# FFN up projections with weights or tokens as the stationary operand

## The chip, the cores and the metric

The kernel runs on one core of a Trainium2 chip. The metric is the device time of one execution in microseconds (us); smaller is better. Before the change it was 1040.62 us, the median of three runs (1040.27 to 1041.07).

## What is computed

Two layers of a decoder trunk, for 256 tokens of 1024 features in float32. Each layer has three sub-layers: an FFN, a token mixer, and another FFN, each behind a norm that a conditioning vector modulates. The FFN is what matters here:

```python
def _swiglu(h, w_up, w_down):          # h [256, 1024], w_up [1024, 2 * 2816], w_down [2816, 1024]
    gu = h @ w_up
    g, u = jnp.split(gu, 2, axis=-1)
    return (jax.nn.silu(g) * u) @ w_down
...
        x = x + 0.5 * gate(0) * _swiglu(norm_mod(x, 0), w_ffn_up[l, 0], w_ffn_down[l, 0])
        x = x + gate(1) * _mixer(norm_mod(x, 1), ...)
        x = x + 0.5 * gate(2) * _swiglu(norm_mod(x, 2), w_ffn_up[l, 1], w_ffn_down[l, 1])
```

## The kernel before

Every float32 matrix product is made of three float32r products: both operands are split into a high part (a cast to float32r) and a low part (what is left), and high x high, high x low and low x high are summed in PSUM. Weights come from HBM in units of 128 x 1024 (`unit`, line 251). ScalarE casts each to `H` (line 247), VectorE subtracts for `L` (line 248). There are 6 buffers for raw units and 11 for split ones. The conditioning (`ada_ss`, `ada_gate`, lines 281 to 323) streams its own weights through VectorE between the chunks of the FFNs.

The normed activations lie transposed in `hTh` and `hTl`: [feature, token tile, feature tile, token], two token tiles of 128.

An FFN has 2816 hidden features, worked on as 11 chunks j of 256. For a chunk and a token tile t, `up(j, t)` (line 466) fills one PSUM bank [128 tokens, 512]: the 256 gate columns and the 256 value columns of the chunk. Its 24 matmuls (8 feature tiles x 3 part products, lines 270 and 272) hold 128 tokens of `hTh` or `hTl` stationary and move 512 weight columns. Silu (line 485) and a product (line 490) give `sg` [128 tokens, 256]. `tr(j, t)` (line 492) transposes it with two matmuls against the identity (line 495, tile `tg`), casts to `gh` (line 498) and subtracts for `gl` (line 499). `down(j, t)` (line 502) then multiplies with two units of down weights: 12 matmuls of 512 columns into two PSUM banks `dn`, which stay open over all chunks (`mm3`, lines 259 to 261). The last chunk's `down` is followed by the residual and the next norm: `norm_sq`, `rsqrt` on GpSimd, `norm_xn` on ScalarE, then transposes `tp` (line 414) and the split of `norm_out`.

In the very first FFN (`pre`), four chunks are begun while the norm's modulation still arrives feature tile by feature tile (line 920); lines 467 to 473 finish them.

The order is written as a list `ops` (lines 523 to 542): an up projection, the transposes of the one before, the down projection of the one before that. At the end it is rearranged so that the first token tile ends early (a = chunk 9, b = chunk 10):

```python
        ops += [(up, (b, 0)), (tr, (a, 1)), (down, (a, 0)), (tr, (b, 0)), (down, (a - 1, 1)), (down, (b, 0)),
                (up, (b, 1)), (tr, (b, 1)), (down, (a, 1)), (lambda *_: after and after[1](0), (0, 0)), (down, (b, 1))]
```

The list is not the order in which the engines work: a scheduler with its own estimate of times orders each engine's queue when the kernel is built, with the list's order as priority. Work that it holds not ready is overtaken by later work. `tc.issue_after(x)` keeps what follows in its block behind x on the engine of x. Each engine then works in order.

Of the kernel before, what the change touches and what calls it, by code (L numbers as in the profile page):

```python
# [9 lines left out]
F32 = mybir.dt.float32  # L10
# [21 lines left out]
# columns of w_in that make up each 512-wide group  # L32
# [7 lines left out]
# tiles of the mixed groups in the order in which they come  # L40
# [33 lines left out]
def _offsets(sizes):  # L74
    at, out = 0, {}
    for name, n in sizes:
# [9 lines left out]
       for n, k in (("cw", 16), ("cb", 4), ("br", 4), ("bi", 4), ("gm", 8), ("wf", 4 * KT))]  # L86
)
CST, N_CST = _offsets([(n, 128) for n in ("ident", "ones", "trif")] + [("fold", 4)]
                       + [(n, 128) for n in ("ntri", "nones", "msb", "mfx")])
# [5 lines left out]
def trunk_kernel(ctx: ExitStack, tc: tile.TileContext, x, c, wst, ada, par, cst, row, bgate, wg, out):  # L95
# [7 lines left out]
    sm = pool("sm", 32)  # L103
    gtp = pool("gtp", 2)
# [26 lines left out]
    # the rows of x, each followed by what adds EPS to its mean square  # L131
# [13 lines left out]
    # -8 * softplus(-lambda), with log1p by its series in e / (2 + e)  # L145
# [27 lines left out]
    # 1/sqrt by two of Newton's steps from a guess on the bits, up to a factor for the user to apply  # L173
# [3 lines left out]
    # the conditioning vector along the rows, and as columns  # L177
# [7 lines left out]
    # for the first norm RS * gain and RS * gain * (1 + bias), by which its scale is one step from its sum  # L185
# [9 lines left out]
    # causal masks next to zeros: [sb | 0 | fox]  # L195
# [4 lines left out]
    def late_constants():  # L200
# [3 lines left out]
        ntri, nones, msb, mfx = (once[:, i * 128:(i + 1) * 128] for i in range(4))  # L204
        S.dma_start(out=r_sb, in_=row.broadcast_to([128, N_ROW]))
        V.tensor_copy(idb, ident)
        for m, n in ((ones_r, C("ones")), (ntri_r, ntri), (nones_r, nones)):
            A.copy(m, n)
# [26 lines left out]
    live = {}  # L235

    # weights not needed at once wait for the norm of the first token tile to be through
# [87 lines left out]
    # in an order in which each is ready when needed, and no gate's row is replaced before its last use  # L325
# [42 lines left out]
    # transposed activations, [feature, token tile, feature tile, token], in their two parts  # L368
# [36 lines left out]
    def norm_out(l, j, t):  # L405
# [4 lines left out]
        for q in range(2):  # L410
# [4 lines left out]
            # one engine per bank  # L415
# [46 lines left out]
    def ffn(l, s, after, pre={}):  # L462
# [3 lines left out]
        def up(j, t):  # L466
            if (j, t) in pre:
                o = pre[j, t]
                wh, wl = unit(("up", l, s, j, KT // 2 - 1))
                for h, w in ((0, wh), (1, wh), (0, wl)):  # L470
                    for i in range(2):
                        T.matmul(o, lhsT=hT[t][h][:, KT - 2 + i, :], rhs=w[:, i * 512:(i + 1) * 512],  # L472
                                 start=False, stop=i == 1 and w is wl)
            else:
                o = PA([128, 512], name="up")
                def w(k):
                    q = slice((k % 2) * 512, (k % 2 + 1) * 512)
                    return [part[:, q] for part in unit(("up", l, s, j, k // 2))]

                if (j, t) == (1, 0):  # L480
                    hold.append(1)
                over_features(o, t, w, (K_T[0 if s else 1], flush) if (j, t) == (1, 0) else None, by=4 if j == 0 else 1)
                hold.clear()
            sg = sgp.tile([128, CH], F32, tag="sg", name="sg")
            silu = act(sg, o[:, 0:CH], AF.Silu)
            prod[j, t] = sg
            if after and (j, t) == (NCH - 1, 1):
                with tc.issue_after(silu.ins):
                    norm_xn(0)
            return V.tensor_tensor(out=sg, in0=sg, in1=o[:, CH:2 * CH], op=ALU.mult)  # L490

        def tr(j, t):
# [7 lines left out]
            gT[j, t] = (gh, gl)  # L500

        def down(j, t):
            if j == 0:
                dn[t] = [PD([128, 512], name="dn") for _ in range(2)]
            gh, gl = gT[j, t]
# [17 lines left out]
        seq = [(0, 0), (1, 0), (0, 1), (1, 1)] + [(j, t) for j in range(2, NCH) for t in range(NT)]  # L523
        if pre:
            seq = [(j, t) for j in range(NCH) for t in range(NT)]
        ops = []
        for i, jt in enumerate(seq):
            ops.append((up, jt))
            if i >= 1:
                ops.append((tr, seq[i - 1]))  # L530
            if i >= 2:
                ops.append((down, seq[i - 2]))
        if pre:
            u, r, d = up, tr, down
            head = [(u, (0, 0)), (u, (0, 1)), (r, (0, 0)), (u, (1, 0)), (r, (0, 1)), (u, (1, 1)), (u, (2, 0)), (u, (2, 1)), (d, (0, 0)), (d, (0, 1)), (r, (1, 0)), (r, (1, 1)), (u, (3, 0)), (d, (1, 0)), (r, (2, 0)), (u, (3, 1)), (d, (1, 1))]
            ops = head + [p for p in ops if p not in head]
        # the first token tile ends early, so that its norm runs under the second's products
        a, b = NCH - 2, NCH - 1
        ops = ops[:ops.index((up, (b, 0)))]
        ops.remove((down, (a - 1, 1)))  # L540
        ops += [(up, (b, 0)), (tr, (a, 1)), (down, (a, 0)), (tr, (b, 0)), (down, (a - 1, 1)), (down, (b, 0)),
                (up, (b, 1)), (tr, (b, 1)), (down, (a, 1)), (lambda *_: after and after[1](0), (0, 0)), (down, (b, 1))]
        for f, jt in ops:
            mul = f(*jt)
            if f is up and jt[1] == 1 and (N_PRE - 1 if pre else 0) < jt[0] < NCH - 1:
                ada_step(ADA_FFN[2 * l + s][jt[0] >= NCH - 4])
            if pre and f is up and jt == (N_PRE, 0):
# [4 lines left out]
    def mixer(l, after):  # L552
# [19 lines left out]
        # RG-LRU: the gelu branch, and the input transposed to [feature, token] with the conv's left margin  # L572
# [12 lines left out]
        # causal conv, gates, log of the decay; two feature tiles at a time  # L585
# [50 lines left out]
            # the queries' scale of HD ** -0.5 goes into the argument  # L636
# [20 lines left out]
        more(fp[:, 4:8], lhsT=C("ones"), rhs=lf[:, 0:4])  # L657
# [15 lines left out]
        # the recurrence  # L673
# [14 lines left out]
        # forgetting attention's scores, [query, key]  # L688
# [34 lines left out]
        # stick-breaking attention  # L723
# [11 lines left out]
        # scores, [key, query], by parity of the head  # L735
# [4 lines left out]
        for e in range(2):  # L740
# [14 lines left out]
            # products with 0 and -1: exact on the two parts  # L755
# [15 lines left out]
        # group norms, then the exact split of the transposed groups  # L771
# [11 lines left out]
        # y of the recurrence: mean square over features by a product with ones  # L783
# [11 lines left out]
        T.matmul(mo, lhsT=C("ones"), rhs=sq[:, 0, :], start=True, stop=True)  # L795
# [11 lines left out]
        # values: [token, head, d]  # L807
# [19 lines left out]
        def values(y, products):  # L827
            """A bank of several sums: the first product opens it, and the others come behind that one."""
# [27 lines left out]
        def finish(t, between=lambda: None):  # L856
            """One bank after the other, so that the residual starts on the first."""
# [23 lines left out]
    # The first layer's shift and scale come feature tile by feature tile, and the first chunks' products  # L881
    # follow them in that order.
# [16 lines left out]
    banks = (PT, PD, PD, PA)  # L899
    for k in range(KT):  # L900
# [9 lines left out]
        for j in range(N_PRE):  # L910
            wh, wl = unit(("up", 0, 0, j, k // 2))
            if k == 1:
                for t in range(NT):
                    pre[j, t] = banks[j]([128, 512], name="up")
            # the parts in the order in which they come about
            for h, w in ((0, wh), (1, wh), (0, wl)):
                for i in range(2):
                    for t in range(NT):
# [101 lines left out]
```

## Time and profile before

| What | Before |
|---|---|
| median of three runs | 1040.62 us |
| the profiled execution, first to last instruction | 1039.9 us |
| instructions | 12805 |
| PE (TensorE matmuls) busy | 1005.7 us, 97% |
| PEld (TensorE weight loads) busy | 803.9 us, 77% |
| DVE (VectorE) busy | 758.1 us, 73% |
| ACT (ScalarE) busy | 534.9 us, 51% |
| bytes read from HBM | 246.15 MB, 238 GB/s over the span |
[...]

PE and PEld are two sides of one engine: a matmul needs its stationary operand loaded, and the load of the next one can run beside the matmul in progress. [...] DVE, ACT and GpSimd (POOL) do everything that is not a matrix product; SP issues the DMAs.

### The profile page before, as it was taken

Reading aid. Unit: us, or ns where it says so; the run is one execution under the profiler, and the core shown is the slowest. Engines: PE = TensorE matmul, PEld = TensorE weight load, DVE = VectorE, ACT = ScalarE, POOL = GpSimd, SP = SyncE. Lnnn points to the kernel's source line nnn. Section 1 sums busy time; section 2 is a strip of 40 time slices with the busy share of each in tenths; the row PEclk is TensorE's granted clock in tenths of the full one; section 3 lists DMA queues with packets and bytes.
Section 4 is the critical chain, followed back from the end, with each engine's and each line's share of the span. In section 5 each row is a group of like instructions: output and inputs, shape, how many; then the busy total and the mean of one; then the engine's idle time right before and its main releaser. Section 6 shows DMA issues by size and latency. Waiting matters only on the chain.

```text
span 1039.9 us, 12805 instructions
## 1 busy us (share of the span) xinstructions
PE 1005.7 (97%) x4542; PEld 803.9 (77%) x4542; DVE 758.1 (73%) x1105; ACT 534.9 (51%) x857; POOL 54.1 (5%) x108
## 2 busy tenths in 40 slices
PE   6999999989999899999999999999999989999998
PEld 4888888768787788888878888887777778888886
DVE  7988877769886797878569887655677559646452
ACT  5473534468775444344455344446679455635340
POOL 1000000120011200000020000001100220000000
PEclk9999999989999999999999999999999999999999
DMA  9989988758473799989539989854542328755511
GB/s 327 375 305 301 339 305 306 263 197 268 148 251 103 242 368 323 318 324 332 195 124 344 337 308 332 311 191 138 184 161 82 101 101 313 272 185 178 187 61 41
DMA packets 68910, 248.04 MB, mean 239 GB/s; under 512 B 7783, under 2 KB 8295, under 8 KB 68846
## 3 DMA queue, kind: packets, MB, share of 16 engines
q1 hardware_dynamic: 68846, 247.23, 67.9%
q8 instruction: 35, 0.57, 0.2%
q14 instruction: 29, 0.24, 0.1%
HBM read 246.15 MB, written 1.05 MB: 238 GB/s over the span
## 4 chain that ended last, share of the span: by engine, by line
PE 82%; ACT 6%; POOL 4%; DVE 4%; issue 3%; DMA 1%; POOLq 0%; ACTq 0%; DVEq 0%
PE up L270 27%; PE up L272 13%; PE dn L259 8%; PE dn L261 8%; PE dn L260 8%; PE pj L270 5%; PE up L920 3%; PE pj L272 2%; PE tg L495 2%; POOL na L359 2%; ACT H L247 2%; POOL ny L360 1%; PE up L472 1%; DVE L L248 1%; PE tp L414 1%
## 5 line engine op out<-in xcount | busy, mean ns | idle before, releaser
L248 DVE TENSOR_TENSOR L<-raw,H 128x1024 fp32r<-128x1024 f32 x320 | 379.0, 1221 | 76.6 <-ACT H L247 74.6
L247 ACT CAST H<-raw 128x1024 fp32r<-128x1024 f32 x320 | 326.8, 1056 | 93.3 <-PE up L272 54.6
L270 PE MATMUL up<-H,hTh 128*128 128x512 f32 x640 | 254.8, 398 | 0.5 <-DVE hTh L427 0.5
L270 PE MATMUL up<-L,hTh 128*128 128x512 f32 x640 | 253.6, 396 | 0.0
L272 PE MATMUL up<-H,hTl 128*128 128x512 f32 x640 | 247.7, 396 | 0.0
L458 ACT ACTIVATE sg<-up 128x256 f32<-128x256 f32 x88 | 33.8, 384 | 242.1 <-PE up L272 237.3
L259 PE MATMUL dn<-H,gh 128*128 128x512 f32 x352 | 146.8, 417 | 2.1 <-ACT gh L498 2.1
L270 PEld LDWEIGHTS up<-H,hTh 128*128 128x128 f32 x640 | 120.9, 189 | 29.5 <-DVE hTh L427 1.3
L272 PEld LDWEIGHTS up<-H,hTl 128*128 128x128 f32 x640 | 120.8, 189 | 29.1
L270 PEld LDWEIGHTS up<-L,hTh 128*128 128x128 f32 x640 | 120.8, 189 | 28.5
L260 PE MATMUL dn<-L,gh 128*128 128x512 f32 x352 | 140.1, 398 | 0.0
L261 PE MATMUL dn<-H,gl 128*128 128x512 f32 x352 | 139.7, 400 | 0.0
L289 DVE SCALAR_TENSOR_TENSOR raw<-raw,cb 128x1024 f32<-128x1024 f32 x96 | 114.2, 1220 | 2.6 <-DMA raw<-in_ada 1.6
L490 DVE TENSOR_TENSOR sg<-sg,up 128x256 f32<-128x256 f32 x88 | 36.9, 420 | 103.7 <-ACT sg L458 103.5
L261 PEld LDWEIGHTS dn<-H,gl 128*128 128x128 f32 x352 | 67.0, 190 | 16.1 <-DVE gl L499 0.2
L259 PEld LDWEIGHTS dn<-H,gh 128*128 128x128 f32 x352 | 66.8, 190 | 15.5 <-ACT gh L498 3.3
L260 PEld LDWEIGHTS dn<-L,gh 128*128 128x128 f32 x352 | 67.3, 191 | 12.9
L270 PE MATMUL pj<-H,hTh 128*128 128x512 f32 x160 | 65.6, 410 | 0.1
L272 PE MATMUL pj<-H,hTl 128*128 128x512 f32 x160 | 65.2, 408 | 0.0
L270 PE MATMUL pj<-L,hTh 128*128 128x512 f32 x160 | 63.9, 399 | 0.0
L312 DVE SCALAR_TENSOR_TENSOR acc<-raw,cs,acc 128x1024 f32<-128x1024 f32 x48 | 61.5, 1283 | 1.1 <-DVE sg L490 0.2
L499 DVE TENSOR_TENSOR gl<-tg,gh 128x256 fp32r<-128x256 f32 x88 | 36.9, 419 | 26.2 <-ACT gh L498 26.2
(252 smaller groups left out, 984.3 us busy)
## 6 DMA issues: line engine op xcount, KB each, us to landing
raw<-in_wst SPq DMA_DIRECT2D x320, 512.0 KB, 5.0
raw<-in_ada SPq DMA_DIRECT2D x144, 512.0 KB, 5.3
x<-in_x SPq DMA_DIRECT2D x2, 512.0 KB, 4.1
wgt<-in_wg SPq DMA_DIRECT2D x2, 512.0 KB
out_x<-x SPq DMA_DIRECT2D x4, 256.0 KB, 2.0
once<-in_cst SPq DMA_DIRECT2D x1, 256.0 KB
p_sb<-in_par SPq DMA_DIRECT2D x1, 148.0 KB
r_sb<-in_row SPq DMA_DIRECT2D x1, 132.0 KB
```

The costliest lines, as they stand in the source:

```text
L247: A.copy(h, raw)
L248: V.tensor_tensor(out=lo, in0=raw, in1=h.bitcast(F32), op=ALU.subtract)
L259: T.matmul(o, lhsT=xh, rhs=wh, start=first, stop=False)
L260: T.matmul(o, lhsT=xh, rhs=wl, start=False, stop=False)
L261: return T.matmul(o, lhsT=xl, rhs=wh, start=False, stop=last)
L270: T.matmul(o, lhsT=hh[:, k, :], rhs=part, start=k == 0 and i == 0, stop=False)
L272: mul = T.matmul(o, lhsT=hl[:, k, :], rhs=w(k)[0], start=False, stop=k == KT - 1)
L289: V.scalar_tensor_tensor(out=raw, in0=raw, scalar=1.0, in1=cb, op0=ALU.mult, op1=ALU.mult, accum_out=st[:, v, k:k + 1])
L312: V.scalar_tensor_tensor(out=acc, in0=raw, scalar=cs[:, m:m + 1], in1=acc, op0=ALU.mult, op1=ALU.add)
L458: used.append(A.activation(*a, **k))
L490: return V.tensor_tensor(out=sg, in0=sg, in1=o[:, CH:2 * CH], op=ALU.mult)
L499: V.tensor_tensor(out=gl, in0=tp, in1=gh.bitcast(F32), op=ALU.subtract)
```

## The change

For most chunks the roles of the operands are exchanged. `up_w(j, i)` holds a 128 x 128 block of weights stationary and moves all 256 tokens: it fills a PSUM bank [128 hidden features, gate and value, 256 tokens], for half i of the chunk's features. It has 48 matmuls (8 feature tiles x 3 part products x gate and value), each of 256 columns. The result is transposed as it comes, so Silu, product, cast and subtraction give `gh` and `gl` [feature, token] without `tr`. `down` is the same but for where it finds its stationary operand.

Chunks 0, 1 and 10 keep `up` and `tr` in three FFNs; in the first FFN only chunk 10 does, and the four early chunks use the new form too. The lists `ops` are written anew, and at the end of an FFN `down(a - 1, 1)` comes ahead of `up(b, 0)`. Two constants (ones, and minus ones) are written by VectorE instead of loaded and copied; the pool `gtp` has 3 buffers for each tag instead of 2, `sm` has 30 instead of 32; the early chunks' PSUM banks come from other pools. `up_w` returns its last matmul where `up` returned VectorE's product, which is what `late_constants` is ordered behind.

```diff
+    def up_part(o, w, kk, v, i, h, k, opens):
+        q = kk * 512 + v * CH + i * 128
+        return T.matmul(o[:, v], lhsT=w[:, q:q + 128], rhs=(hTh, hTl)[h][:, :, k, :], start=opens, stop=True,
+                        skip_group_check=True)
...
+        def up_w(j, i):
+            if (j, i) in pre:
+                o = pre[j, i]
+                wh, wl = unit(("up", l, s, j, KT // 2 - 1))
+                for h, w in ((0, wh), (1, wh), (0, wl)):
+                    for kk in range(2):
+                        for v in range(2):
+                            mul = up_part(o, w, kk, v, i, h, KT - 2 + kk, False)
+            else:
+                o = PA([128, 2, SEQ], name="up")
+                with ExitStack() as behind:
+                    for k in range(KT):
+                        wh, wl = unit(("up", l, s, j, k // 2))
+                        for h, w in ((0, wh), (0, wl), (1, wh)):
+                            for v in range(2):
+                                opens = k == 0 and h == 0 and w is wh and v == 0
+                                mul = up_part(o, w, k % 2, v, i, h, k, opens)
+                                if opens:
+                                    behind.enter_context(tc.issue_after(mul.ins))
+            sg = sgp.tile([128, SEQ], F32, tag="sg", name="sg")
+            act(sg, o[:, 0], AF.Silu)
+            V.tensor_tensor(out=sg, in0=sg, in1=o[:, 1], op=ALU.mult)
+            gh = gtp.tile([128, NT, 128], F32R, tag="gh", name="gh")
+            gl = gtp.tile([128, NT, 128], F32R, tag="gl", name="gl")
+            sg = sg.rearrange("p (t q) -> p t q", t=NT)
+            A.copy(gh, sg)
+            V.tensor_tensor(out=gl, in0=sg, in1=gh.bitcast(F32), op=ALU.subtract)
+            for t in range(NT):
+                gT[j, i, t] = (gh[:, t], gl[:, t])
+            return mul
...
-                mm3(dn[t][n], gh[:, i, :], gl[:, i, :], w[i][0][:, q], w[i][1][:, q],
+                mm3(dn[t][n], *gT[j, i, t], w[i][0][:, q], w[i][1][:, q],
...
+        u, w, r, d = up, up_w, tr, down
         if pre:
+            ops = [(w, (0, 0)), (w, (0, 1)), (w, (1, 0)), (w, (1, 1)), (d, (0, 0)), (w, (2, 0)), (d, (0, 1)),
+                   (w, (2, 1)), (d, (1, 0)), (w, (3, 0)), (d, (1, 1)), (w, (3, 1)), (w, (4, 0)), (d, (2, 0)),
+                   (d, (2, 1)), (w, (4, 1)), (d, (3, 0)), (d, (3, 1))]
+        else:
+            ops = [(u, (0, 0)), (u, (1, 0)), (r, (0, 0)), (u, (0, 1)), (r, (1, 0)), (d, (0, 0)), (u, (1, 1)),
+                   (r, (0, 1)), (d, (1, 0)), (w, (2, 0)), (r, (1, 1)), (d, (0, 1)), (w, (2, 1)), (d, (1, 1))]
         a, b = NCH - 2, NCH - 1
+        for j in range(5 if pre else 3, a):
+            ops += [(w, (j, 0)), (d, (j - 1, 0)), (w, (j, 1)), (d, (j - 1, 1))]
+        ops += [(w, (a, 0)), (d, (a - 1, 0)), (w, (a, 1)), (d, (a - 1, 1)), (u, (b, 0)), (d, (a, 0)), (r, (b, 0)),
+                (d, (b, 0)), (u, (b, 1)), (r, (b, 1)), (d, (a, 1)), (lambda *_: after and after[1](0), (0, 0)),
+                (d, (b, 1))]
         for f, jt in ops:
             mul = f(*jt)
...
-            if pre and f is up and jt == (N_PRE, 0):
+            if f is up_w and pre and jt == (N_PRE, 0):
                 with tc.issue_after(mul.ins):
                     late_constants()
...
-    banks = (PT, PD, PD, PA)
+    banks = (PD, PD, PT, PA)
...
-            for h, w in ((0, wh), (1, wh), (0, wl)):
                 for i in range(2):
-                    for t in range(NT):
-                        kk = k - 1 + i
-                        T.matmul(pre[j, t], lhsT=hT[t][h][:, kk, :], rhs=w[:, i * 512:(i + 1) * 512],
-                                 start=kk == 0 and w is wh and h == 0, stop=kk == KT - 1 and w is wl)
+                    pre[j, i] = banks[j]([128, 2, SEQ], name="up")
+            with ExitStack() as behind:
+                for h, w in ((0, wh), (1, wh), (0, wl)):
+                    for kk in range(2):
+                        for v in range(2):
+                            for i in range(2):
+                                opens = k == 1 and h == 0 and w is wh and kk == 0 and v == 0
+                                mul = up_part(pre[j, i], w, kk, v, i, h, k - 1 + kk, opens)
```

## Rows read from the trace of the kernel before

**Rows 1.** The page: busy us of an engine, share of the span, instructions.
```profile
span 1039.9 us, 12805 instructions
...
PE 1005.7 (97%) x4542; PEld 803.9 (77%) x4542; DVE 758.1 (73%) x1105; ACT 534.9 (51%) x857; POOL 54.1 (5%) x108
```

**Rows 2.** Table by windows: length, busy us and starts by engine, clock, DMA, GB/s.
```profile
26.00:54.00 28.00, 28.00 (x122) 22.72 (x121) 27.66 (x49) 13.10 (x17) 0.00 (x0) 1.00 1.00 377
...
80.00:132.00 52.00, 52.00 (x230) 41.90 (x229) 45.57 (x78) 21.97 (x31) 0.00 (x0) 1.00 0.92 316
```

**Rows 3.** Waits, 80 to 185 us: who waited for whom, us, times, longest.
```profile
ACT sg L458 <- PE up L272: 52.3, 12, 8.0
```

**Rows 4.** Groups by shape, whole run: busy us, mean ns, idle us before.
```profile
L495 PE MATMUL tg<-c_sb,sg 128*128 128x128 f32 x176 | 33.4, 272 | 0.0
...
L229 PE MATMUL s<-mask,idb 128*128 128x512 bf16 x6 | 1.6, 383 | 0.0
```

**Rows 5.** Timeline of PE, first FFN: start us, length us, line, tiles, count.
```profile
61.96 0.40 PE L259 MATMUL dn<-H,gh 128*128 128x512 f32 x1
...
65.94 0.40 PE L261 MATMUL dn<-H,gl 128*128 128x512 f32 x1
...
123.67 0.38 PE L495 MATMUL tg<-c_sb,sg 128*128 128x128 f32 x2
...
132.29 0.38 PE L495 MATMUL tg<-c_sb,sg 128*128 128x128 f32 x2
```

**Rows 6.** Timeline of PE and PEld, 100 to 104 us.
```profile
100.15 0.39 PE L270 MATMUL up<-L,hTh 128*128 128x512 f32 x1
100.15 0.19 PEld L272 LDWEIGHTS up<-H,hTl 128*128 128x128 f32 x1
...
103.88 0.39 PE L272 MATMUL up<-H,hTl 128*128 128x512 f32 x1
```

**Rows 7.** Timeline of PE, mixer of layer 0: first and last `fo`, then masks.
```profile
259.68 0.28 PE L622 MATMUL fo<-hTh,wfs 128*8 128x256 f32 x1
...
261.40 0.28 PE L623 MATMUL fo<-hTl,wfs 128*8 128x256 f32 x1
261.52 0.82 PE L229 MATMUL s<-mask,idb 128*128 128x512 bf16 x3
```

**Rows 8.** Timeline of PEld, mixer of layer 1: loads ahead of 64-column matmuls.
```profile
809.73 0.53 PEld L831 LDWEIGHTS yfx<-vt,pTb 128*128 128x128 f32 x4
810.18 0.30 PEld L831 LDWEIGHTS yfx<-vt,pTa 128*128 128x128 f32 x2
```

**Rows 9.** Timeline of PE, mixers: float32r matmuls of 256 columns and their successors.
```profile
290.58 0.28 PE L232 MATMUL zb<-gl,ntri_r 128*128 128x256 f32 x1
290.69 0.28 PE L232 MATMUL za<-gl,nones_r 128*128 128x256 f32 x1
290.81 0.40 PE L232 MATMUL za<-ah,ntri_r 128*128 128x512 f32 x1
...
796.99 0.28 PE L232 MATMUL za<-gl,nones_r 128*128 128x256 f32 x1
797.11 0.39 PE L232 MATMUL za<-ah,ntri_r 128*128 128x512 f32 x1
```

**Rows 10.** Timelines around FFN ends, PE and ACT; in brackets idle us, releaser.
```profile
192.86 0.38 PE L495 MATMUL tg<-c_sb,sg 128*128 128x128 f32 x2
...
195.85 0.38 ACT L498 CAST gh<-tg 128x256 fp32r<-128x256 f32 x1
...
199.19 0.40 PE L261 MATMUL dn<-H,gl 128*128 128x512 f32 x1
...
209.98 0.66 PE L414 MATMUL tp<-c_sb,xn 128*128 128x128 f32 x4 [2.51 <-ACT xn L403]
...
525.02 1.04 PE L414 MATMUL tp<-c_sb,xn 128*128 128x128 f32 x8
```

More of the change, by code (lines that the diff above doesn't have):

```diff
@@ L87 @@
 )
-CST, N_CST = _offsets([(n, 128) for n in ("ident", "ones", "trif")] + [("fold", 4)]
-                       + [(n, 128) for n in ("ntri", "nones", "msb", "mfx")])
+CST, N_CST = _offsets([(n, 128) for n in ("ident", "trif")] + [("fold", 4)]
+                       + [(n, 128) for n in ("ntri", "msb", "mfx")])
 N_RES = CST["ntri"][0]
@@ L102, in trunk_kernel @@
     w2 = pool("w2", 5)
-    sm = pool("sm", 32)
-    gtp = pool("gtp", 2)
+    sm = pool("sm", 30)
+    gtp = pool("gtp", 3)
     sgp = pool("sgp", 3)
@@ L203, in late_constants @@
         S.dma_start(out=once, in_=cst[:, N_RES:])
-        ntri, nones, msb, mfx = (once[:, i * 128:(i + 1) * 128] for i in range(4))
+        ntri, msb, mfx = (once[:, i * 128:(i + 1) * 128] for i in range(3))
         S.dma_start(out=r_sb, in_=row.broadcast_to([128, N_ROW]))
         V.tensor_copy(idb, ident)
-        for m, n in ((ones_r, C("ones")), (ntri_r, ntri), (nones_r, nones)):
-            A.copy(m, n)
+        V.memset(ones_r.bitcast(F32), 1.0)
+        V.memset(nones_r.bitcast(F32), -1.0)
+        A.copy(ntri_r, ntri)
         V.tensor_copy(mask[:, 0, :], msb)
@@ L466, in up, with w @@
         def up(j, t):
-            if (j, t) in pre:
-                o = pre[j, t]
-                wh, wl = unit(("up", l, s, j, KT // 2 - 1))
-                for h, w in ((0, wh), (1, wh), (0, wl)):
[L471 to L483, printed above, removed]
+            o = PA([128, 512], name="up")
+            def w(k):
+                q = slice((k % 2) * 512, (k % 2 + 1) * 512)
+                return [part[:, q] for part in unit(("up", l, s, j, k // 2))]
+            if (j, t) == (1, 0):
+                hold.append(1)
+            over_features(o, t, w, (K_T[0 if s else 1], flush) if (j, t) == (1, 0) else None, by=4 if j == 0 else 1)
+            hold.clear()
             sg = sgp.tile([128, CH], F32, tag="sg", name="sg")
@@ L499, in tr @@
             V.tensor_tensor(out=gl, in0=tp, in1=gh.bitcast(F32), op=ALU.subtract)
-            gT[j, t] = (gh, gl)
+            for i in range(2):
+                gT[j, i, t] = (gh[:, i], gl[:, i])
         def down(j, t):
@@ L521, in down @@
                     pending.append(lambda: after[1](1))
-        seq = [(0, 0), (1, 0), (0, 1), (1, 1)] + [(j, t) for j in range(2, NCH) for t in range(NT)]
+        u, w, r, d = up, up_w, tr, down
         if pre:
[L525 to L536, printed above, removed]
-        a, b = NCH - 2, NCH - 1
[L539 to L542, printed above, removed]
+            ops = [(w, (0, 0)), (w, (0, 1)), (w, (1, 0)), (w, (1, 1)), (d, (0, 0)), (w, (2, 0)), (d, (0, 1)),
[4 more added lines that the diff above has]
+                   (r, (0, 1)), (d, (1, 0)), (w, (2, 0)), (r, (1, 1)), (d, (0, 1)), (w, (2, 1)), (d, (1, 1))]
@@ L543, in ffn @@
+        a, b = NCH - 2, NCH - 1
+        for j in range(5 if pre else 3, a):
[3 more added lines that the diff above has]
+                (d, (b, 1))]
         for f, jt in ops:
             mul = f(*jt)
-            if f is up and jt[1] == 1 and (N_PRE - 1 if pre else 0) < jt[0] < NCH - 1:
+            if f in (up, up_w) and jt[1] == 1 and (N_PRE - 1 if pre else 0) < jt[0] < NCH - 1:
@@ L656, in mixer @@
         T.matmul(fp, lhsT=C("trif"), rhs=lf, start=True, stop=False, skip_group_check=True)
-        more(fp[:, 4:8], lhsT=C("ones"), rhs=lf[:, 0:4])
+        more(fp[:, 4:8], lhsT=ones_r.bitcast(F32), rhs=lf[:, 0:4])
         qaT = W4([66, 4, SEQ], name="qaT")
@@ L794, in mixer @@
         mo = PT([128, SEQ], name="mo")
-        T.matmul(mo, lhsT=C("ones"), rhs=sq[:, 0, :], start=True, stop=True)
+        T.matmul(mo, lhsT=ones_r.bitcast(F32), rhs=sq[:, 0, :], start=True, stop=True)
         rl = W2([128, SEQ], name="rl")
@@ L912, in trunk_kernel @@
             if k == 1:
-                for t in range(NT):
-                    pre[j, t] = banks[j]([128, 512], name="up")
-            for h, w in ((0, wh), (1, wh), (0, wl)):
                 for i in range(2):
-                    for t in range(NT):
-                        kk = k - 1 + i
-                        T.matmul(pre[j, t], lhsT=hT[t][h][:, kk, :], rhs=w[:, i * 512:(i + 1) * 512],
-                                 start=kk == 0 and w is wh and h == 0, stop=kk == KT - 1 and w is wl)
+                    pre[j, i] = banks[j]([128, 2, SEQ], name="up")
[3 more added lines that the diff above has]
+                        for v in range(2):
+                            for i in range(2):
+                                opens = k == 1 and h == 0 and w is wh and kk == 0 and v == 0
+                                mul = up_part(pre[j, i], w, kk, v, i, h, k - 1 + kk, opens)
+                                if opens:
+                                    behind.enter_context(tc.issue_after(mul.ins))
     for l in range(DEPTH):
@@ L987, in _pack @@
     consts = {
-        "ident": np.eye(128), "ones": np.ones((128, 128)), "ntri": -1.0 * ~(i[:, None] < i[None, :]),
-        "nones": -np.ones((128, 128)), "trif": le, "msb": np.where(i[:, None] < i[None, :], 0.0, -1e30),
+        "ident": np.eye(128), "ntri": -1.0 * ~(i[:, None] < i[None, :]),
+        "trif": le, "msb": np.where(i[:, None] < i[None, :], 0.0, -1e30),
         "mfx": np.where(i[None, :] <= i[:, None], 0.0, -1e30), "fold": i[:, None] % 4 == np.arange(4)[None, :],
```

1 line of the change is left out of this document (removed).

## The prediction

> **What bounds the kernel now.** I read the page's busy times first: the tensor engine (PE) is busy 97% of a span of 1039.9 us, its weight loads 77% [rows 1]. Busy time overlaps on this engine (a matmul of 0.39 us is followed by the next after 0.23 us [rows 6]), so I looked at starts, not durations. The stages come from the table by windows: from 26 to 54 us the DMA engines are full (1.00, 377 GB/s), VectorE is busy 27.66 of 28.00 us and PE is full too; from 80 to 132 us PE is full, VectorE at 45.57 of 52.00 us, DMA at 0.92 [rows 2]. That PE sets the pace in the FFNs is told by the waits: from 80 to 185 us ScalarE's Silu waited 52.3 us for the up projection, in 12 waits, the longest sum of that stretch [rows 3]. So what changes on PE in the FFNs reaches the end of the kernel nearly one to one, as long as the others keep up.
>
> **What is removed: transposes.** There are 176 `tg` transposes, two in each of 88 calls of `tr` [rows 4]. The change keeps `tr` for chunks 0, 1 and 10 of three FFNs and chunk 10 of the first: 10 chunks, 20 calls. So 34 chunks change, and 68 calls go. Their price is what they add to PE's rhythm, not their duration of 272 ns: two successive `tg` pairs start at 123.67 and 132.29, 8.62 us apart, with 24 up and 12 down matmuls and one pair between [rows 5]. An up matmul takes (103.88 - 100.15) / 16 = 0.2331 us [rows 6], a down one (65.94 - 61.96) / 17 = 0.2341 us [rows 5]. 8.62 - 24 x 0.2331 - 12 x 0.2341 = 0.217 us for a call. 68 x 0.217 = 14.8 us go from PE. The copies behind them stay (one Silu, product, cast and subtraction for each 128x256 tile, as before, now out of SBUF); their producers have slack [rows 3], so I take their change as nothing. If that cover were gone, each would lie open with some 0.4 us (`gh`: 0.38) [rows 10], but their reader comes a whole `up_w` later (48 matmuls, 5.6 us).
>
> **What is added: narrower matmuls.** A chunk had 48 up matmuls of 512 moving columns; now it has 96 of 256, the same columns but twice as many weight loads. In 34 chunks 1632 wide ones become 3264 narrow ones. Everything hangs on the time from one narrow matmul to the next, and it has two floors.
> The moving side: `fo` moves exactly the new operand (256 tokens of `hTh` or `hTl` in two pieces) past a load of 8 columns; 16 of them start from 259.68 to 261.40, that is 1.72 / 15 = 0.1147 us each [rows 7]. Two of them are 0.2294 us, a little under one wide matmul.
> The load side: the next 128x128 load starts with the running matmul (both at 100.15) [rows 6]. Where matmuls are short (64 columns), loads alone set the pace: four start from 809.73 to 810.18, 0.1125 us each, although each is recorded as 0.19 us long [rows 8]. Recorded lengths overlap; 0.1125 just fits under 0.1147.
> Both at once: the stick-breaking scores hold a few matmuls of 256 columns with a 128x128 float32r load on either side. Those at 290.58 and 290.69 take 0.23 us together, that at 796.99 takes 0.12 us [rows 9]; (0.23 + 0.12) / 3 = 0.1167. There are seldom two in a row, so how a long run of them goes isn't shown. I take 0.117, since they have the same form. Bounds are 0.1147 [rows 7] and 0.12, the slowest of the three [rows 9]: (2 x 0.117 - 0.2331) x 1632 = +1.5 us, with ends of -6.0 and +11.3 us. Break-even with the 14.8 us is at 0.1211.
> [...]
>
> **What is moved.** At the end of an FFN, `down(a-1, 1)` stood between the last transposes of token tile 0 and `down(b, 0)`, which needs their copy; it now comes before the last chunk's up projection. Today those transposes are at 192.86, the cast `gh` on ScalarE only at 195.85, the last matmul of `down(b, 0)` at 199.19, and the next norm's transposes at 209.98 after 2.51 us of idle PE [rows 10]. With `down(a-1, 1)` gone from there, `gh` is waited for right away. The scheduler fills such holes with the up projection behind it, so PE works on; but what it fills with is then missing as cover for the norm. `tr` to the end of `down(b, 0)` is 6.6 us now; after the change a transpose pair (0.2), the cast of 0.38 us with its hand-overs (together 1.0 to 1.5, an estimate) and 12 matmuls (2.8) make 4.0 to 4.5, while 2.8 come ahead of it: 2.8 + 4.0 to 4.5 - 6.6 = +0.2 to +0.7 us, where the norm is waited for. That is so in the two handovers from FFN to mixer, and not between the layers, where the norm's transposes at 525.02 followed without idle time [rows 10]; +1.0 us together. The other end is the cast being held up as long as now (3.0 us) in all three: 3 x 2.8 = +8.4 us. Below nothing: at most the 2.51 us of idle. The last FFN has no norm behind it.
> The order of the first FFN's head changes too (`up_w(4, 0)` ahead of `down(2, 0)`), but PE had no hole there, and as much work stands behind each need: nothing, or part of rival C. `late_constants` is no longer ordered behind VectorE's product of chunk 4 (`up_w` returns a matmul, so the ordering binds PE alone). Its small VectorE steps may come earlier; VectorE's queue holds other chunks' splits behind them, which are ready ahead: nothing. The constants left out and the pools' sizes carry no time.
>
> **Sum.** -14.8 + 1.5 + 1.0 = -12.3 us on the profiled span of 1039.9, thus 1027.6. The median of the runs, 1040.62, is 0.7 above that span; with it 1028.3 us.
>
> **Rivals.**
> A, the forecast, 1028.3. Its own range, with the narrow matmul between 0.1147 and 0.12 and the handovers between -2.5 and +1.0, is 1017 to 1038. 72%.
> B, slower: the extra time of a float32r matmul belongs to the load beside it, not to its columns. A bf16 matmul of the same 512 columns takes (0.82 - 0.383) / 2 = 0.2185 us [rows 7, 4], the float32r one 0.2331 [rows 6], 0.0146 more. If each load costs that, 1632 more loads cost 23.8 us, and the narrow matmul takes 0.124: 1040.6 - 14.8 + 1.0 + 23.8 = 1050.6. For it: loads will run nearly without a break (0.1125 of each 0.117 us), which no long stretch of this trace shows. Against it: `fo` has nearly no load and is as slow per column [rows 7], and the three narrow ones lie under 0.1211, from which B decides [rows 9]. 11%.
> C, another engine takes over in the first FFN, where DMA and VectorE are nearly full [rows 2]: its 20 calls (10 chunks) of 0.217 us, 4.3 us, are not gained: 1032.6. Against it: Silu's waits for PE [rows 3], and a chunk that is 0.4 of 17.2 us shorter asks only 2.5% more of them. 8%.
> D, the handovers cost the upper end of 8.4 us: 1035.7. For it: `gh` did stand behind a weight cast on ScalarE. 7%.
> E, loads don't hide at all behind matmuls of the same rows. A narrow pair would take 0.1125 + 0.1147 = 0.227 us: 3264 x 0.227 - 1632 x 0.2331 = +361 us, some 1388. Against it: the load lies inside the matmul's time [rows 6], and three narrow ones took 0.1167 [rows 9]. 2%.
> [...]
> That the code doesn't do what it says (wide matmuls stay) I see no room for: `up_part` issues 128-column slices by itself.
>
> **How the numbers follow.** A is likeliest: 1028.3. The range of 1018 to 1037 takes in A but for its tails, C and D, and leaves out B and E. What a measurement of this kernel can tell from no change is about 0.2%, 2 us: 1038.5 to 1042.7 counts as the same. Slower is B and E but for B's mild half-cases (0.12); same is what lies between, slow ends of A and D (0.05); faster the rest (0.83).
>
> **What would show it.** In the profile after, the up projection has 3264 matmuls of 256 columns, 480 of 512, and 40 `tg`; up matmuls start 0.117 us apart in a long run (0.124 for B, 0.227 for E); a chunk in the middle of an FFN lasts 17.24 - 0.43 + 48 x 0.0009, about 16.85 us. The weight loads' busy sum goes beyond the span (804 + 1632 x 0.19 is 1114 us) without being the bound. If PE waits for ScalarE's `H` or VectorE's `L` in the first FFN, C was right; if the idle time ahead of the norm's transposes (2.51 us) grows by over 2 us, D. A mean distance of over 0.121 us makes the prediction wrong in sign.

## The result and the profile after

The changed kernel took 1033.66 us (median of seven executions, 1031.17 to 1037.18) where the kernel before took 1040.27 beside it: ratio 0.9932, 95% interval 0.9911 to 0.9954. That is 6.6 us faster; 12.3 were forecast. Two later measurements, on two chips, gave 1032.67 against 1040.25 and 1032.5 against 1040.56. The forecast's sign and range held, the size did not: about a third to a half of the gain is missing, and the rest of this document looks for it.

The page of the changed kernel (busy us, share of the span, instructions), against [rows 1]:

```profile
span 1029.4 us, 15807 instructions
PE 994.3 (97%) x6038; PEld 871.8 (85%) x6038; DVE 759.9 (74%) x1107; ACT 538.1 (52%) x855; POOL 53.3 (5%) x108
```

PE lists 1496 instructions more (1632 matmuls more, 136 transposes fewer), and is as full as before. The table by windows (length, busy us and starts by engine, granted clock, DMA share, GB/s), against [rows 2]:

```profile
26.00:54.00 28.00, 28.00 (x239) 28.00 (x238) 27.89 (x57) 11.98 (x16) 0.00 (x0) 1.00 0.98 366
80.00:132.00 52.00, 52.00 (x356) 48.04 (x355) 44.92 (x53) 24.41 (x33) 0.00 (x0) 1.00 0.94 328
```

PE has no hole in either window. Its loads now run almost throughout (28.00 of 28.00 us, 48.04 of 52.00), VectorE and DMA stand as they did. Who waited for whom from 80 to 185 us, against [rows 3]:

```profile
ACT sg L459 <- PE up L467: 40.9, 11, 7.0
```

ScalarE still waits for the up projection, so PE still sets the pace there. The groups by shape (busy us, mean ns, idle us before), against [rows 4], with the narrow matmul as a new line; two more groups of 1088 stand beside it:

```profile
L467 PE MATMUL up<-hTh,H 128*128 128x256 f32 x1088 | 211.0, 282 | 3.7 <-ACT H L248 3.7
...
L271 PE MATMUL up<-H,hTh 128*128 128x512 f32 x160 | 64.2, 401 | 0.4 <-DVE hTh L428 0.4
```

3 x 1088 = 3264 narrow matmuls and 3 x 160 = 480 wide ones: the code does what the forecast said. The idle 3.7 us ahead of the narrow ones is one wait, at the start of the kernel, and will matter.

Two stretches of PE's timeline: a long run of narrow matmuls, listed in pairs, against [rows 6], and the first down matmul of each of three half chunks later on, where [rows 5] had two transposes a half chunk apart:

```profile
100.18 0.40 PE L467 MATMUL up<-hTh,H 128*128 128x256 f32 x2
...
104.92 0.28 PE L467 MATMUL up<-hTl,H 128*128 128x256 f32 x1
...
386.55 0.40 PE L260 MATMUL dn<-H,gh 128*128 128x512 f32 x1
...
395.04 0.40 PE L260 MATMUL dn<-H,gh 128*128 128x512 f32 x1
...
403.52 0.40 PE L260 MATMUL dn<-H,gh 128*128 128x512 f32 x1
```

40 narrow matmuls start between the first two rows: 4.74 / 40 = 0.1185 us each. Over all that follow one another from 25 us on, the mean is 0.1186, the same in all four FFNs. A half chunk takes 8.49 us where it took 8.62 [rows 5], so a chunk takes 16.97 us (403.52 - 386.55); 16.85 was forecast.

Where the 10.5 us between the two profiled executions lie (starts of PE's instructions; a stretch ends where the next begins):

| stretch | before, us | after, us | difference |
|---|---|---|---|
| start to the first up matmul | 16.90 | 18.40 | +1.50 |
| first FFN, to its last down matmul | 200.46 | 197.02 | -3.44 |
| first mixer, to the first down matmul behind it | 136.98 | 135.84 | -1.14 |
| second and third FFN, first to last down matmul | 370.95 | 366.38 | -4.57 |
| second mixer, to the first down matmul behind it | 136.43 | 135.81 | -0.62 |
| fourth FFN, first to last down matmul | 173.27 | 171.00 | -2.27 |
| end | 4.91 | 4.92 | +0.01 |

The FFNs gained 10.28 us, the start lost 1.50. The mixers' 1.76 us are not of the change; the fourth group of experiments shows where such differences come from.

### The profile page after: what moved, and what is told of

It is laid out like the page before. It is cut to its first block, busy times and chain, and to the rows that moved or that the text cites. A ratio compares the mean times of both kernels' runs of the same rounds, so it can differ in the third digit from the quotient of the medians.

```text
span 1029.4 us, 15807 instructions
## 1 busy us (share of the span) xinstructions
PE 994.3 (97%) x6038; PEld 871.8 (85%) x6038; DVE 759.9 (74%) x1107; ACT 538.1 (52%) x855; POOL 53.3 (5%) x108
## 4 chain that ended last, share of the span: by engine, by line
PE 83%; ACT 6%; POOL 4%; DVE 3%; issue 2%; DMA 1%; SPq 0%; DVEq 0%; POOLq 0%; ACTq 0%
PE up L467 38%; PE dn L260 8%; PE dn L262 8%; PE dn L261 8%; PE up L271 5%; PE pj L271 5%; PE up L273 3%; PE pj L273 2%; ACT H L248 2%; POOL na L360 1%; PE wo L260 1%; PE wo L261 1%; PE wo L262 1%; POOL ny L361 1%; PE tp L415 1%
## 5 line engine op out<-in xcount | busy, mean ns | idle before, releaser
L467 PE MATMUL up<-hTh,H 128*128 128x256 f32 x1088 | 211.0, 282 | 3.7 <-ACT H L248 3.7
L467 PE MATMUL up<-hTl,H 128*128 128x256 f32 x1088 | 211.9, 283 | 0.0
L467 PE MATMUL up<-hTh,L 128*128 128x256 f32 x1088 | 211.3, 282 | 0.0
L467 PEld LDWEIGHTS up<-hTh,H 128*128 128x128 f32 x1088 | 169.2, 189 | 9.9 <-ACT H L248 4.1
L467 PEld LDWEIGHTS up<-hTl,H 128*128 128x128 f32 x1088 | 165.1, 189 | 0.0
L467 PEld LDWEIGHTS up<-hTh,L 128*128 128x128 f32 x1088 | 164.4, 189 | 0.0
L260 PE MATMUL dn<-H,gh 128*128 128x512 f32 x352 | 141.1, 401 | 1.6 <-ACT gh L532 1.6
L290 DVE SCALAR_TENSOR_TENSOR raw<-raw,cb 128x1024 f32<-128x1024 f32 x96 | 114.0, 1220 | 2.1 <-DMA raw<-in_ada 2.1
L516 DVE TENSOR_TENSOR sg<-sg,up 128x256 f32<-128x256 f32 x68 | 28.5, 419 | 66.0 <-ACT sg L459 65.7
L271 PE MATMUL up<-H,hTh 128*128 128x512 f32 x160 | 64.2, 401 | 0.4 <-DVE hTh L428 0.4
L271 PE MATMUL up<-L,hTh 128*128 128x512 f32 x160 | 63.1, 395 | 0.0
```

Source lines behind the costliest of these rows:

```text
L260: T.matmul(o, lhsT=xh, rhs=wh, start=first, stop=False)
L271: T.matmul(o, lhsT=hh[:, k, :], rhs=part, start=k == 0 and i == 0, stop=False)
L290: V.scalar_tensor_tensor(out=raw, in0=raw, scalar=1.0, in1=cb, op0=ALU.mult, op1=ALU.mult, accum_out=st[:, v, k:k + 1])
L467: return T.matmul(o[:, v], lhsT=w[:, q:q + 128], rhs=(hTh, hTl)[h][:, :, k, :], start=opens, stop=True, skip_group_check=True)
L516: V.tensor_tensor(out=sg, in0=sg, in1=o[:, 1], op=ALU.mult)
```

## The experiments

My theory had two parts: the narrow matmul takes 0.1186 us and not 0.117, which is a cost of its weight load; and the start lost 1.5 us because the late constants had lost their hold. The rivals: the transposes were worth less than thought, the handovers took the difference, or the order of the first chunks delayed the start.

### The two halves of the change apart

The first kernel is the one before with the transposes of the 68 calls left out; the copies behind them read the product as it lies, so the down projections get operands that aren't transposed.

```diff
         def tr(j, t):
-            tp = PT([128, 2, 128], name="tg")
-            for i in range(2):
-                T.transpose(tp[:, i, :], prod[j, t][:, i * 128:(i + 1) * 128], ident)
+            if j < NCH - 1 and (pre or j > 1):
+                tp = prod[j, t].rearrange("p (i q) -> p i q", i=2)
+            else:
+                tp = PT([128, 2, 128], name="tg")
+                for i in range(2):
+                    T.transpose(tp[:, i, :], prod[j, t][:, i * 128:(i + 1) * 128], ident)
```

> The kernel before with the transposes of the same 68 calls of tr left out (cast and subtraction read sg itself, so the down projection is fed data in the wrong layout); up projections stay wide. If a call costs the 0.217 us that the rhythm of the kernel before showed: 14.8 us less than before, some 1025.5 us, ratio 0.986. If other waits take their place: less than 10 us gained. A chunk should last 17.25 - 0.43 = 16.82 us.

The second is the changed kernel with two transposes behind each narrow up projection of the three later FFNs (48 calls), and the copies behind them; it transposes what needs no transposing.

```diff
+        def tr_w(j, i):
+            sg = prod[j, i, "w"]
+            ...
+                tp = PT([128, NT, 128], name="tg")
+                for t in range(NT):
+                    T.transpose(tp[:, t, :], sg[:, t * 128:(t + 1) * 128], ident)
...
+            ops.append((f, jt))
+            if late:
+                ops.append((tr_w, late.pop()))
```

> The changed kernel with two transposes put back behind each narrow up projection of the three later FFNs (24 chunks, 48 calls; the result is transposed once too often, so its output is wrong); the first FFN is as in the changed kernel. If the two parts add up: 48 x 0.217 = 10.4 us slower than the changed kernel, so 1043 to 1044 us, ratio to before 1.003; chunks of the later FFNs 16.97 + 0.43 = 17.40 us, 0.15 longer than before (the price of narrowness alone). If narrow matmuls cost nothing: 17.25 us.

Measured: without the transposes 1022.43 us (ratio 0.9826, 0.9796 to 0.9856), narrow with transposes 1044.63 (ratio 1.0028, 1.0005 to 1.0051). The times also hold the start and the mixers, so I go by the second and third FFN, from their first to their last down matmul. PE's timeline of the four kernels at these two points (start us, length us): before,

```profile
354.34 0.48 PE L259 MATMUL dn<-H,gh 128*128 128x512 f32 x1
...
725.29 0.40 PE L261 MATMUL dn<-H,gl 128*128 128x512 f32 x1
```

after,

```profile
351.26 0.48 PE L260 MATMUL dn<-H,gh 128*128 128x512 f32 x1
...
717.64 0.39 PE L262 MATMUL dn<-H,gl 128*128 128x512 f32 x1
```

without the transposes,

```profile
346.77 0.48 PE L259 MATMUL dn<-H,gh 128*128 128x512 f32 x1
...
710.62 0.40 PE L261 MATMUL dn<-H,gl 128*128 128x512 f32 x1
```

and narrow with transposes:

```profile
357.34 0.48 PE L260 MATMUL dn<-H,gh 128*128 128x512 f32 x1
...
731.22 0.39 PE L262 MATMUL dn<-H,gl 128*128 128x512 f32 x1
```

370.95, 366.38, 363.85 and 373.88 us. These two FFNs hold 16 of the 34 chunks. Without the transposes they are 7.10 us shorter, the fourth FFN (8 chunks) 3.57: 10.67 us for 48 calls, 0.222 us a call. The forecast had 0.217. So the transposes were worth what was thought, and that rival falls. The narrow matmuls with transposes are 2.93 us longer than before, in the fourth FFN 1.63: 4.56 / 24 = 0.19 us a chunk, 6.5 us for 34 chunks. By its own rhythm it is (2 x 0.1186 - 0.2331) x 1632 = 6.7 us. Two ways to the same size, where the forecast had 1.5.

### What the narrow matmul's extra time is

The narrow matmuls with loads of 64 columns, but for the first of each accumulation; half of the hidden features of these projections are left out.

```diff
+        m = 128 if first else 64
-        return T.matmul(o[:, v], lhsT=w[:, q:q + 128], rhs=(hTh, hTl)[h][:, :, k, :], start=opens, stop=True,
+        return T.matmul(o[0:m, v], lhsT=w[:, q:q + m], rhs=(hTh, hTl)[h][:, :, k, :], start=opens, stop=True,
```

> The changed kernel with weight loads of 64 columns instead of 128 in the narrow matmuls, but for the first of each accumulation; half of the hidden features are left out, the moving side is unchanged. The narrow matmul took 0.1186 us in the changed kernel. If the weight load beside it sets or lengthens that time (rival B in part): it falls to between 0.1146 (what fo showed) and 0.1165. If the moving columns alone set it: it stays at 0.1186.

Measured: one execution of 1025.73 us. PE's timeline, the same stretch as above:

```profile
99.93 0.39 PE L468 MATMUL up<-hTh,H 128*64 128x256 f32 x2
...
103.20 0.40 PE L468 MATMUL up<-hTl,H 128*64 128x256 f32 x2
```

28 matmuls in 3.27 us, 0.1168 each; over the whole trace from 25 us on 0.1166. Halving the load takes 2.0 of the 118.6 ns away. That is not the load's whole price: 0.1166 is half of a wide matmul (0.2331), but the wide one has a 128-column load beside it too, once for 512 columns. A pair of narrow matmuls, with one load more than a wide one, measures 2 x 0.1186 - 0.2331 = 0.0041 us more, and 1632 x 0.0041 = 6.7 us is what the narrow form costs. Past loads of 8 columns, the 20 stretches of `fo` in the ten profiles took 0.1140 to 0.1147 us a matmul, but 0.1169 in four of them; so beside 256 columns a 128-column load costs between 1.7 and 4.6 ns by these rows. Rival B named this mechanism, with a price of 14.6 ns for each additional load.

One rival is left. This run halves the width of the result too (64 partitions of PSUM and not 128), and a cost that grows with that width would look the same; no run here parts the two. That the load matters at all, the next run shows.

Then the other side: 128 moving columns and not 256, but for the first of each accumulation, so that the load is nearly as long as the matmul is now; half the tokens of these projections are left out.

```diff
+        n = slice(0, NT if first else 1)
-        return T.matmul(o[:, v], lhsT=w[:, q:q + 128], rhs=(hTh, hTl)[h][:, :, k, :], start=opens, stop=True,
+        return T.matmul(o[:, v, 0:128 * n.stop], lhsT=w[:, q:q + 128], rhs=(hTh, hTl)[h][:, n, k, :], start=opens,
```

> The changed kernel with 128 moving columns in each narrow matmul and not 256, but for the first of each accumulation; half the tokens of these projections are left out. If the load of 128 columns is hidden behind the matmul and costs only its 2 ns, the pace falls with the columns, to about 0.0583 + 0.002 = 0.060 us. If a load takes TensorE's load side about 0.112 us (the pace of the loads that follow each other in the trace of before), it sets the pace as soon as the matmul is shorter: 0.11 to 0.115 us, hardly below the 0.1186 us of 256 columns, and the whole is then only 3264 x 0.005 = 16 us shorter instead of 3264 x 0.058 = 190.

Measured: one execution of 1091.62 us, 58 us longer with half of the columns; neither theory had that. PE's timeline in the first FFN, at the end of its long run of up projections, and in the second:

```profile
86.33 1.05 PE L468 MATMUL up<-hTh,H 128*128 128x128 f32 x4
87.18 1.05 PE L468 MATMUL up<-hTl,H 128*128 128x128 f32 x4
...
91.98 0.63 PE L261 MATMUL dn<-L,gh 128*128 128x512 f32 x1
92.41 0.63 PE L262 MATMUL dn<-H,gl 128*128 128x512 f32 x1
...
93.64 0.39 PE L262 MATMUL dn<-H,gl 128*128 128x512 f32 x1
93.87 0.39 PE L260 MATMUL dn<-H,gh 128*128 128x512 f32 x1
...
443.11 0.38 PE L468 MATMUL up<-hTh,L 128*128 128x128 f32 x2
443.33 0.39 PE L468 MATMUL up<-hTl,H 128*128 128x128 f32 x2
...
456.88 0.63 PE L468 MATMUL up<-hTh,H 128*128 128x128 f32 x2
457.30 0.63 PE L468 MATMUL up<-hTh,L 128*128 128x128 f32 x2
```

And two windows of the same execution (columns as above; the clock is the third number from the end):

```profile
30.00:84.00 54.00, 54.00 (x255) 54.00 (x255) 40.41 (x62) 20.96 (x26) 0.00 (x0) 1.00 0.85 308
455.70:468.00 12.30, 12.30 (x54) 11.89 (x53) 9.51 (x17) 4.58 (x6) 0.00 (x0) 0.50 0.94 339
```

Two rhythms alternate. At 443 us two matmuls take 0.22 us; 42 of them start from 441.99 to 446.68 us, 0.1117 each: hardly less than the 0.1186 of 256 columns, and close to the loads' own pace of 0.1125 in [rows 8]. By these numbers the load sets the pace here, as the second theory had it, though a load is listed as 0.19 us long.

At 457 us two take 0.42 to 0.43 us (42 start from 456.45 to 465.41 us, 0.2133 each), where the granted clock is 0.50. From 19.7 to 91.5 us the matmuls have that same rhythm (0.85 us for four), and so do the first wide ones behind them (0.43 us each) until, with wide ones running, they go to 0.23 at 93.64. The windows' column says 1.00 from 30 to 84 us; the rhythm says otherwise, and I go by the rhythm. The start of the changed kernel has the same disagreement: its window from 18.40 to 24.00 us says 1.00, yet eight narrow matmuls take 1.70 us there (from 20.28 to 21.98) and 0.95 later (from 26.57 to 27.52). In that trace the first record of the clock is at 23.7 us, where the rhythm changes: for the time before, the column has none to go by. So with 128 columns PE kept for 72 us, without a hole in its list, the rhythm that goes with a granted clock of 0.50 at 457 us, and left it among 512-column matmuls. From the first up to the first down matmul that took 71.7 us where the changed kernel took 42.4. The rest of the 58 lies in later stretches in that rhythm, such as the one from 452.79 us on, behind 4.27 us of idle PE (its wide matmuls take 0.42 to 0.43 us each), and in idle time itself: PE's busy time is 1028.8 of 1089.8 us, 61.0 us idle, where the changed kernel has 35.1. How much belongs to which I did not part. With 256 columns the changed kernel's first FFN is at 0.1186 from 25 us on.

### The lost hold

The changed kernel with one word different: the narrow up projection hands back its VectorE product, and not its last matmul, so that the late constants are held behind a VectorE instruction again.

```diff
-            V.tensor_tensor(out=sg, in0=sg, in1=o[:, 1], op=ALU.mult)
+            prod_v = V.tensor_tensor(out=sg, in0=sg, in1=o[:, 1], op=ALU.mult)
...
-            return mul
+            return prod_v
```

> The changed kernel with one word different: the narrow up projection hands back its product on VectorE and not its last matmul, so that the late constants are held behind a VectorE instruction again, as before the change. Theory (losing that hold let some twenty small VectorE instructions of the late constants in among the split of the first weights, and delayed the first up projection): the first up matmul at 16.9 us of the span and not 18.4, TensorE's idle time there 2.7 us and not 3.7, and the whole 1.5 us shorter than the changed kernel, about 1031.2 us. Rival (the start is late because the banks of the first chunks or their order changed, and the hold is only beside it): the first up matmul stays at 18.4 and the time at that of the changed kernel.

And the kernel before without its hold:

```diff
-                with tc.issue_after(mul.ins):
-                    late_constants()
+                late_constants()
```

> The kernel before with one edit: the late constants are no longer held behind the product of the first later chunk. Theory of the lost hold: the first up matmul goes from 16.9 us to about 18.4 and the whole is 1.5 us longer, about 1041.8 us. Rival (first chunks' banks and order): the first up matmul stays at 16.9 and the time at that of before, 1040.3 us.

Beside them, the changed kernel once more:

> [...]

Measured: 1031.42 us with the hold restored (1028.58 to 1032.94; ratio 0.9898, 0.9873 to 0.9923), 1032.5 for the changed kernel on the same chip (ratio 0.9923, 0.9897 to 0.9948), 1042.96 for the kernel before without its hold (ratio 1.0019, 0.9999 to 1.0038). Both edits go the expected way, by 1.1 and 2.4 us, but the intervals don't part them from their partners; the place does. VectorE's timeline of the changed kernel, 9 to 13 us (start us, length us; five more steps of L219 and L220 stand among them):

```profile
9.67 0.20 DVE L214 RECIPROCAL n<-n 128x8 f32<-128x8 f32 x1
...
11.63 0.17 DVE L220 TENSOR_SCALAR n<-n 128x8 f32<-128x8 f32 x1
11.71 1.23 DVE L290 SCALAR_TENSOR_TENSOR raw<-raw,cb 128x1024 f32<-128x1024 f32 x1
```

and with the hold restored:

```profile
9.25 0.21 DVE L361 TENSOR_SCALAR ny<-na,ny 128x1 f32<-128x1 f32 x1
9.99 1.23 DVE L290 SCALAR_TENSOR_TENSOR raw<-raw,cb 128x1024 f32<-128x1024 f32 x1 [0.53 <-ACT cb L183]
```

L214 to L220 are the late constants' little series; each step is short, but together they hold L290, the first conditioning product, whose scale the first activations wait for. ScalarE's row that completes `cb`, the conditioning vector that L290 reads, in the changed kernel and with the hold restored:

```profile
9.69 0.58 ACT L183 ACTIVATE cb<-pc 128x512 f32<-128x512 f32 x1
```

```profile
9.38 0.58 ACT L183 ACTIVATE cb<-pc 128x512 f32<-128x512 f32 x1
```

In the changed kernel `cb` is complete at 10.27 us and L290 starts 1.44 us later. With the hold VectorE sits idle for `cb` and starts L290 0.03 us after it. PE's first up matmul, in the changed kernel, with the hold restored, and in the kernel before without its hold:

```profile
18.40 2.08 PE L467 MATMUL up<-hTh,H 128*128 128x256 f32 x8 [3.75 <-ACT H L248]
```

```profile
16.68 2.08 PE L467 MATMUL up<-hTh,H 128*128 128x256 f32 x8 [2.72 <-ACT H L248]
```

```profile
18.12 1.22 PE L919 MATMUL up<-H,hTh 128*128 128x512 f32 x2 [3.75 <-ACT H L247]
```

Before, it stood at 16.90, and in the changed kernel's three profiles at 17.97 to 18.42. The idle time goes between 2.72 and 3.75 with the hold. From the start of L290 to the first up matmul it is 6.68 to 6.69 us in all ten profiles, so whatever delays L290 delays PE by as much. L290 starts 0.03 us behind `cb` in the three profiles that have the hold (before, restored, without the transposes), 1.01 to 1.48 us behind it in six of the seven that have not, and 2.72 in that of 128 moving columns. In the first two profiles that is 1.41 of the 1.50 us; `cb` itself was complete 0.09 us later. The order of the first chunks and their banks is the same with the hold restored, so that rival falls. Part of the delay is made up before the first down matmul: there the restored hold is 0.9 to 1.4 us ahead of the changed kernel's three profiles, 1.1 in the mean, and the kernel before is 1.0 ahead of itself without the hold. So I put the lost hold at 1.1 us.

### The changed kernel again

> The changed kernel itself, to see how far its executions scatter. In the first comparison they lay between 1031.2 and 1037.2 us, those of the kernel before (but for one) between 1039.3 and 1041.1. Theory 1 (the saving is a steady 0.28 us in each of 34 chunks, and the rest is scatter): ratio to before 0.991 to 0.994, and a chunk in the middle of an FFN lasts 2 x 8.487 us again. Theory 2 (something in the new form is slow in some executions alone): chunks of another length than 16.97 us in a slower execution's profile.

Measured: 1032.67 us (1029.95 to 1035.36; ratio 0.9918, 0.9892 to 0.9945), with the same half chunk of 8.487 us and the first up matmul at 18.42. From the first mixer's projections to its output projections it took 90.90 us where the first profile took 88.55. One place of that: windows around the norm's transposes ahead of the mixer, and the transposes themselves, first in this execution, then in the first one:

```profile
226.00:228.60 2.60, 2.07 (x9) 1.98 (x10) 0.18 (x1) 1.94 (x5) 0.00 (x0) 0.64 1.02 400
...
226.53 1.84 PE L415 MATMUL tp<-c_sb,xn 128*128 128x128 f32 x8 [2.59 <-ACT xn L404]
```

```profile
226.00:228.60 2.60, 1.81 (x12) 1.68 (x13) 0.67 (x3) 2.27 (x6) 0.00 (x0) 1.00 1.00 410
...
226.79 1.10 PE L415 MATMUL tp<-c_sb,xn 128*128 128x128 f32 x8 [1.92 <-ACT xn L404]
```

Behind 2.59 us of idle PE the granted clock is 0.64 on average and eight transposes take 1.84 us; behind 1.92 us it is 1.00 and they take 1.10. Both kernels have such places: from the first mixer's last output projection to the first down matmul behind it took 23.0 us in the profile of before and 21.5 in that of the same kernel without its hold. So 1 to 2 us of the difference between two single executions can be such stretches. What sets the idle time ahead of them from one execution to the next I did not settle.

## Why the prediction was right, and where it missed

- **PE sets the pace in the FFNs, nearly one to one: right.** Two FFNs got 4.57 us shorter, and 16 chunks that are each 2 x (8.627 - 8.487) = 0.28 us shorter make 4.48.
- **Transposes, -14.8 us: right.** Leaving them out gave 0.222 us a call, 68 of which make 15.1. (The subtraction in the prediction comes to 0.216 and not 0.217, which moves its term by 0.1 us.)
- **The narrow matmul, +1.5 us: the mis-sized term.** It measured 0.1186 us, inside the bounds of 0.1147 to 0.12 but not at the 0.117 taken, and the term is +6.7 us. The step that failed is "(0.23 + 0.12) / 3 = 0.1167", with "I take 0.117, since they have the same form" [rows 9]. Three starts that are written to 0.01 us fix a matmul to some 0.003 us, and with 3264 of them 0.003 us is 10 us. All that the rows gave was the bounds; their middle, (0.1147 + 0.12) / 2 = 0.1174, would have made +2.8, and the long run came out still nearer to the slow end.
- **Rival B: the mechanism fits, the price was wrong.** An additional load costs 4.1 ns with its matmul, not 14.6. B took the whole difference between float32r and bf16 for the load; but two `fo`, each with a load of 8 columns, take 0.2294 us [rows 7] where the bf16 matmul takes 0.2185, so most of that difference is in the moving side.
- **Rival E: wrong here.** Loads of all 128 rows lay under matmuls of the same rows: the matmuls follow one another at 0.1186 us, where a load and a matmul one after the other would take 0.1125 + 0.1147 = 0.227, and in the profile after the pair of loads listed from 100.30 us starts within the pair of matmuls listed from 100.18 us for 0.40 us.
- **Handovers, +1.0 us: not seen.** The second and third FFN, which hold the handover between the layers and the end ahead of the second mixer, are explained by their chunks to 0.1 us. Ahead of the first mixer the idle time is a little shorter than the 2.51 us of [rows 10]:

```profile
208.44 1.11 PE L415 MATMUL tp<-c_sb,xn 128*128 128x128 f32 x4 [2.31 <-ACT xn L404]
```

  Rival D falls with it. The work that now fills the hole was as good a cover.
- **Late constants, "nothing": wrong, +1.1 us** (1.4 at the first up matmul, of the 1.50 by which the profile's start grew). The step that failed is "VectorE's queue holds other chunks' splits behind them, which are ready ahead: nothing". I looked for the steps in the middle of the first FFN. Without the hold they went to the very start, ahead of VectorE's first long products, where PE waits for the chain through VectorE and ScalarE and nothing covers it.
- **Rival C: not seen.** No row lists PE waiting from 26 to 60 us, and the first FFN gained 3.44 us where its ten chunks alone make 10 x 0.28 = 2.8.
- **A small gain not foreseen:** down matmuls take 0.2327 us and not 0.2341, 816 of them in the changed chunks: -1.1 us. In the kernel before without its transposes they took 0.2338, and with the loads of 64 columns, where the operands' layout is the new one too, 0.2336; so the layout alone does not bring it. What does, no run here parts.
- **A sign that could not show:** the prediction had the loads' busy sum go beyond the span, at 1114 us. The lengths of the 6038 loads do add up to 1128 us, but the profile's page counts overlapping loads once: 871.8.

With measured terms the sum is -15.1 + 6.7 - 1.1 + 1.1 = -8.4 us. The medians of the three measurements are 6.6, 7.6 and 8.1 us shorter than those of before. The profiled executions differ by 10.5, of which 1.8 lie in the mixers. So the sum stands within 1.8 us of each median, and no further term is needed. That the forecast missed by no more than 4 to 6 us is in part luck: the handovers' +1.0 that did not come and the lost hold's +1.1 that was not forecast cancel, and the faster down matmuls (-1.1) pay for part of the mis-sized term.

## What to carry to other kernels

Swapping the operands to save a transpose paid here because the additional loads stayed under the matmuls (0.1186 us for a matmul with its load, not 0.227). Each of them still cost 4.1 ns with its matmul; multiply such a price by their count before taking the transposes' price as the gain. A term of many thousand equal instructions needs their rhythm to a nanosecond, from a long run; three rows are a bound and not a value. And when a function hands back another engine's instruction than before, look at what was ordered behind it: here the lost hold let small work go to the start of the kernel, where L290 started 1.44 us behind `cb` and not 0.03, on the chain that PE waits for.

## What the runs showed of the hardware

- With 128 moving columns and a 128-column load for each matmul, a stream of matmuls had a rhythm of 0.1117 us (442 to 447 us of that execution), near the 0.1125 of loads that follow each other [rows 8]; with 256 columns the changed kernel has 0.1186. Half the moving columns took 6.9 ns from a matmul there.
- In the one execution taken, such a stream also ran for 72 us at 0.2133 us a matmul, the rhythm it had at a granted clock of 0.50 at 457 us, with PE listed as busy without a break, and left it among wide matmuls. Later, at 442 us, the same stream came in at 0.1117 and kept it to its end at 447. Why the first did not change before, no run here shows. The window's clock column said 1.00 all the while; only the distance between starts showed the rhythm.
- Beside loads of 128 columns, matmuls of 256 columns take 0.1186 us, beside 64 columns (and half the result's width) 0.1166, beside 8 columns 0.1140 to 0.1169, though the loads of the changed kernel (189 ns as listed) start while a matmul (282 ns) runs.
